# A hybrid encoder block: gate-up weight sums all formed at once, another order of its seven products, and an output projection in 512 columns

## The chip, the cores and the metric

The kernel runs on one core of a Trainium2 chip. The metric is the device time of one execution in microseconds (us), the median of the runs shown. The engines are named TensorE (PE), VectorE (DVE), ScalarE (ACT), GpSimd (POOL) and SyncE (SP, which here only issues DMAs).

## The reference

One layer of a trunk, on x of 2048 tokens by 1024 channels, everything in float32:

```python
h  = rms_norm(x, norm_mix)
u  = h @ w_in                                   # (2048, 2560): lru_x, lru_g, q, k, v of 512 each
y_lru = gelu(lru_g) * rg_lru(conv4(lru_x), ...) # a gated linear recurrence over time
y_att = stick_breaking_attention(q, k, v)       # 8 heads of 64, causal, no softmax
y  = concat([rms_norm(y_lru), rms_norm(y_att)])
x  = x + y @ w_out                              # output projection, 1024 x 1024
h2 = rms_norm(x, norm_ffn)
gu = h2 @ w_ffn_in                              # gate-up projection, 1024 x 5632
x  = x + (silu(gu[:, :2816]) * gu[:, 2816:]) @ w_ffn_out   # down projection
out = rms_norm(x, norm_final)
```

## The kernel before

**Precision.** Each operand of a large product is split into a high part (`hi`, a cast by ACT to the type fp32r) and a low part (`lo`, source minus `hi`, a subtraction by DVE or POOL). `mm3` (L149 to L151) then issues three multiplications for each block: hi by hi, hi by lo, lo by hi. A split therefore always means a cast on ACT and a subtraction on DVE or POOL (`split` with its flag `pool`).

**Stages.** The span runs through these stages. First, for each of four groups of 512 tokens, the input projection of the next group goes on beside the attention of the present one (`drive` hands steps of the one between steps of the other). In the last group, from 801 to 1208 us, the output projection of all groups takes the place of the input projection (`mix_out`, class `Mix`); its last part, the tail, runs after attention, to about 1242. In the tail the tokens for the gate-up projection are prepared too (`prep_tokens`, L801). Then the gate-up projection (44 quads, about 1250 to 2172), and then the down projection to the end.

**Output projection.** `Mix.run` (L657) takes, for each 512 columns of the output, two half blocks of weights from `next_half`. A half is 256 columns wide and holds all four channel blocks of a branch. For each of four token tiles it fills one bank of PSUM, left half and then right half, in 8 x 3 multiplications of 256 columns; it yields four times on the way, so that attention steps can come between.

**Gate-up by Strassen's scheme.** Weights and tokens are cut into 2 x 2 blocks (a11, a12, a21, a22 and b11, b12, b21, b22, where the first index of a and b runs over outputs and channels of the scheme), and seven products of sums replace eight. The weight sums are s1 to s4, the token sums t1 to t4; `ORDER` (L64) pairs them and sets the order of the products. Each product is 4 row blocks x 3 multiplications of 512 columns, in one of four banks a to d (each with two buffers). Of one `quad`: product 0 (a11, b11) goes to bank a and is copied out by ACT as p; a later product is added on top of it in bank a and copied out as u; DVE adds u to bank c as the second u ("u3" in the code); and bank c and then d are filled further after DVE has read them. `use` adds a bank and one of the copies into an activation tile c; for the even quads ACT applies silu to it, for the odd ones DVE multiplies it with the gate of the quad before, and POOL forms five sums of such tiles (e), which go to DRAM (act_d) as operands of the down projection.

**Weights of the next quad.** `prep_weights` (L893) is a generator. `done(i)`, called after product i of the present quad, lets it take one step for the next quad. Its six steps: the split of the first raw block (a11 and a12 together, 1024 wide, subtraction on POOL); the sums s3 and s1, and the split of s3 (POOL); the sum s2 and its split (DVE); the split of s1 (DVE); the split of a22 (POOL) and the sum s4, formed in place in s2; the split of s4 (POOL) and the issue of the loads of the quad after (`load_weights`, two raw blocks of 512 KB, L885). There is one pair of raw buffers, so the next load starts when their last reader is through. Split weights live in a ring of six buffers (`WSB`), a11 and a12 in two double-width ones.

**Tokens.** `EARLY` names the five token operands that are prepared in the tail; the other two follow in the gate-up stage, ahead of the first quad. `turns_late` prepares the second half of the tokens beside the first half's quads: transposes on PE, and sums t1 to t4 on POOL that go to DRAM. At the swap of halves `split_tokens` loads and splits 7 x 4 token tiles, each after the product that used the old one.

**Order of the work.** PE's instructions are issued in the order of the program (`manual_schedule`). The other engines, and SP, get an order from a planner, which takes the instruction that is ready first by its own estimate of times, and among ready ones the one that stands first in the program. On the chip every engine then works in that order, whatever really comes first: an instruction that waits holds all behind it.

## Time and profile before

| | |
|---|---|
| time, median of 3 runs | 2612.49 us (2610.23 to 2614.08) |
| profiled execution | 2616.12 us, of which the span of instructions is 2614.4 us |
| PE, matmul | 2417.2 us busy, 92% |
| PE, weight load | 2046.0 us busy, 78% |
| DVE | 1837.1 us busy, 70% |
| ACT | 1258.0 us busy, 48% |
| POOL | 1174.2 us busy, 45% |
| DMA | 468.57 MB, mean 179 GB/s |
| granted clock of TensorE, mean | 0.970 |

A clock of 1.00 is 2.4 GHz; the other level is 1.2 GHz, and a value between them is a mean over time at both. A busy share is an average over stages with different limits, so the rows below are taken by stretch of time (us from the start of the span). Multiplications are pipelined: one of 512 columns is recorded with 0.39 us, but the next one starts well before that has passed, so the step from start to start is what counts.

### The profile page before, as it was taken

The page shows a single profiled execution, that of the slowest core. Times are in us where ns is not written, and L with a number is a line of the kernel's source. Part 1 is how long each engine was busy: PE and PEld are TensorE (multiplying, and loading weights), DVE is VectorE, ACT ScalarE, POOL GpSimd, SP SyncE. Part 2 cuts the span into 40 slices and gives each one's busy share as a digit, 9 for nine tenths or more (in the row PEclk, how much of TensorE's full clock was granted, in tenths as well). Part 3 has the DMA queues.
Part 4 walks back from the last instruction along what each step waited for, and adds up shares of the span by engine and source line. Part 5 has one row for each costly group of instructions (what it writes and reads, how often), then busy time and mean ns, then how long its engine had stood idle before and what let it go on. Part 6 is the DMA issues. An engine that isn't in the chain of part 4 may idle for free.

```text
span 2614.4 us, 36856 instructions
## 1 busy us (share of the span) xinstructions
PE 2417.2 (92%) x12680; PEld 2046.0 (78%) x12680; DVE 1837.1 (70%) x2569; ACT 1258.0 (48%) x2277; POOL 1174.2 (45%) x1397
## 2 busy tenths in 40 slices
PE   7999999998888887998799979979999999999998
PEld 5888788787778787888577758868888887788886
DVE  4566888999999999898645546686566562544557
ACT  5656677676766665665433323343333332332334
POOL 5855433223244221112565565464555454644443
PEclk9999999999999999999899989989999999999999
DMA  7787887664556565654333453252332326755563
GB/s 254 254 289 254 268 264 228 197 210 164 163 182 204 176 200 174 218 177 138 128 133 129 150 196 110 90 199 89 109 113 93 102 92 263 272 174 173 195 200 145
DMA packets 221804, 468.57 MB, mean 179 GB/s; under 512 B 22704, under 2 KB 63664, under 8 KB 221616
## 3 DMA queue, kind: packets, MB, share of 16 engines
q1 hardware_dynamic: 221616, 466.21, 53.1%
q8 instruction: 100, 1.64, 0.3%
q14 instruction: 88, 0.72, 0.1%
HBM read 333.74 MB, written 132.38 MB: 178 GB/s over the span
## 4 chain that ended last, share of the span: by engine, by line
PE 43%; DVE 3%; DMA 2%; POOL 2%; issue 2%; ACT 1%; SPq 0%; POOLq 0%; DVEq 0%; ACTq 0%
PE pw L151 5%; PE pw L150 5%; PE pw L149 5%; PE psc L149 3%; PE psa L149 3%; PE psc L150 3%; PE psc L151 3%; PE psa L150 3%; PE psa L151 3%; PE psd L149 3%; PE psd L150 3%; PE psd L151 3%; PE psb L149 1%; PE psb L150 1%; PE psb L151 1%
## 5 line engine op out<-in xcount | busy, mean ns | idle before, releaser
L360 POOL MEMSET u<- 128x1 f32 x320 | 31.2, 99 | 558.0 <-DVE u L372 393.4
L372 DVE TENSOR_TENSOR_SCAN u<-u,u,zero 128x513 f32<-128x513 f32 x192 | 255.5, 1332 | 9.0 <-ACT u L362 8.5
L393 PE MATMUL t<-ident,be 128*128 128x128 f32 x1088 | 180.2, 282 | 55.2 <-DVE al L395 46.2
L378 DVE TENSOR_TENSOR be<-be,u 128x512 f32<-128x512 f32 (+2 forms) x320 | 215.2, 675 | 17.0 <-POOL be L366 1.4
L362 ACT ACTIVATE u<-z 128x512 f32<-128x512 f32 (+2 forms) x320 | 172.4, 539 | 96.8 <-PE z L358 61.2
L149 PE MATMUL pj<-ht_hi,w_hi 128*128 128x512 f32 x512 | 214.9, 420 | 2.3 <-DVE sl L291 1.5
L394 ACT CAST ah<-t 128x512 fp32r<-128x512 f32 (+2 forms) x320 | 168.7, 527 | 87.0 <-PE t L393 81.6
L393 PEld LDWEIGHTS t<-ident,be 128*128 128x128 f32 x1088 | 131.7, 144 | 94.1 <-DVE al L395 60.5
L151 PE MATMUL pj<-ht_hi,w_lo 128*128 128x512 f32 x512 | 202.3, 395 | 0.0
L150 PE MATMUL pj<-ht_lo,w_hi 128*128 128x512 f32 x512 | 202.0, 395 | 0.0
L358 PE MATMUL z<-ks,qd 128*128 128x512 f32 (+2 forms) x640 | 191.1, 380 | 6.8 <-ACT be L363 5.2
L395 DVE TENSOR_TENSOR al<-t,ah 128x512 fp32r<-128x512 f32 (+2 forms) x320 | 191.1, 598 | 7.1 <-ACT ah L394 6.7
L1089 POOL TENSOR_TENSOR e<-c,c 128x512 f32<-128x512 f32 x110 | 158.7, 1451 | 50.5 <-DVE c L1080 36.8
L363 ACT ACTIVATE be<-z 128x512 f32<-128x512 f32 (+2 forms) x320 | 172.6, 539 | 0.2
L408 PE MATMUL y<-ah,vs 128*128 128x256 f32 x576 | 149.6, 290 | 13.9 <-DVE yp L418 13.9
L149 PE MATMUL po<-wo_hi,yhi 128*128 128x256 f32 x512 | 156.3, 305 | 0.0
L372 DVE TENSOR_TENSOR_SCAN u<-u,zero 128x129 f32<-128x129 f32 (+3 forms) x128 | 112.1, 877 | 57.0 <-POOL u L366 55.4
L1142 DVE TENSOR_TENSOR blo<-dr,bhi 128x1024 fp32r<-128x1024 f32 (+1 forms) x41 | 83.1, 2029 | 94.5 <-ACT bhi L1141 94.5
L1142 POOL TENSOR_TENSOR a0lo<-act,a0hi 128x1024 fp32r<-128x1024 f32 (+1 forms) x41 | 99.4, 2424 | 110.6 <-ACT a0hi L1141 110.6
L408 PE MATMUL y<-al,vs 128*128 128x256 f32 x576 | 147.2, 286 | 0.0
L150 PE MATMUL po<-wo_lo,yhi 128*128 128x256 f32 x512 | 146.6, 286 | 0.0
L151 PE MATMUL po<-wo_hi,ylo 128*128 128x256 f32 x512 | 146.6, 286 | 0.0
(283 smaller groups left out, 7564.3 us busy)
## 6 DMA issues: line engine op xcount, KB each, us to landing
r<-in_w_gu SPq DMA_DIRECT2D x88, 512.0 KB, 4.1
act<-act_d SPq DMA_DIRECT2D x68, 512.0 KB, 4.1
dr<-in_w_dn SPq DMA_DIRECT2D x59, 512.0 KB, 4.5
act_d<-e SPq DMA_DIRECT2D x110, 256.0 KB, 2.0
w_hi<-w_d SPq DMA_DIRECT2D x50, 512.0 KB, 4.7
w_lo<-w_d SPq DMA_DIRECT2D x50, 512.0 KB, 5.6
vs<-vs_d SPq DMA_DIRECT2D x80, 256.0 KB, 3.6
ks<-ks_d SPq DMA_DIRECT2D x80, 256.0 KB, 3.6
```

Source lines behind the costliest of these rows:

```text
L149: nc.tensor.matmul(ps, lhsT=w_hi, rhs=m_hi, start=first, stop=False, skip_group_check=more)
L150: nc.tensor.matmul(ps, lhsT=w_hi, rhs=m_lo, start=False, stop=False, skip_group_check=more)
L151: nc.tensor.matmul(ps, lhsT=w_lo, rhs=m_hi, start=False, stop=last, skip_group_check=more)
L358: nc.tensor.matmul(z[:, :nz], lhsT=qd[:, i, qs], rhs=kss[p.c][:, :nz], start=i == 0, stop=i == 1)
L362: nc.scalar.activation(u[:, :n], z[:, :n], AF.Sigmoid, scale=-SCALE)
L363: nc.scalar.activation(be[:, :n], z[:, :n], AF.Sigmoid, scale=SCALE)
L372: nc.vector.tensor_tensor_scan(out=ur, data0=ur, data1=zero.broadcast_to([P, n + 1]), initial=1.0 if p.prev is None else p.prev.u[s][:, 0: ...
L378: nc.vector.tensor_tensor(out=p.be[s][:, :n], in0=p.be[s][:, :n], in1=p.u[s][:, 1:n + 1], op=ALU.mult)
L393: nc.tensor.transpose(tp[:, b, :], p.be[s][:, b * P:(b + 1) * P], ident)
L395: nc.vector.tensor_tensor(out=alo[:, :nb, s, :], in0=tp[:, :nb, :], in1=f32(ahi[:, :nb, s, :]), op=ALU.subtract)
L408: nc.tensor.matmul(y, lhsT=vs[:, b, :], rhs=t[:, b].rearrange("p s q -> p (s q)"), start=first and m == 0, stop=last and m == 1)
L1142: eng.tensor_tensor(out=lo, in0=src, in1=f32(hi), op=ALU.subtract)
```

## The change

The weight sums of a quad are formed in the first two steps of `prep_weights` instead of over five of them; a22 gets buffers of its own and is split in the second step, and the loads of the quad after are issued there too. The products come in another order: the one that takes a12 and b21 is now second, in bank b, and its `use` follows at once. b21 changes places with t4 in `EARLY`: t4 is formed in the tail, stored to DRAM, and loaded and split later. For the very first quad a11 and a12 are loaded and split at the end of the tail, in buffers of the pool of token tiles. Pools: split weights 6 to 5 buffers (and two new ones for a22), weight sums 3 to 4, copies p/u 3 to 2, activation tiles 8 to 6. In the output projection a half of the weights is 512 columns by two channel blocks instead of 256 by four, and a multiplication has 512 columns. The raw loads of w_in and w_out are written with flat patterns.

```diff
-WSB = 6
-CB = 8
+WSB = 5
+CB = 6
-ORDER = (("a11", "b11"), ("s3", "t3"), ("s2", "t2"), ("s1", "t1"), ("a22", "t4"), ("s4", "b22"), ("a12", "b21"))
-EARLY = ("b11", "t1", "t2", "t3", "t4")
+ORDER = (("a11", "b11"), ("a12", "b21"), ("s3", "t3"), ("s2", "t2"), ("s1", "t1"), ("a22", "t4"), ("s4", "b22"))
+EARLY = ("b11", "b21", "t3", "t2", "t1")
...
     def run(self, x2, following=None, ready=NCT):
             for n in range(D // GT):
-                halves = [next_half(), next_half()]
+                halves = [[w.rearrange("p (a k) c -> p a (k c)", a=2) for w in next_half()] for _ in range(2)]
...
-                    for i, (hi, lo) in enumerate(halves):
-                        for c in range(NCT):
-                            yh, yl = self.split[c]
-                            mm3(po[:, i * WC:(i + 1) * WC], yh[:, ts], yl[:, ts], hi[:, c], lo[:, c],
-                                c == 0, c == NCT - 1)
-                            if c == 1 or (c == NCT - 1 and i == 0):
-                                yield
+                    for c in range(NCT):
+                        yh, yl = self.split[c]
+                        hi, lo = halves[c // 2]
+                        mm3(po, yh[:, ts], yl[:, ts], hi[:, c % 2], lo[:, c % 2], c == 0, c == NCT - 1)
+                        if c < NCT - 1:
+                            yield
...
@@ prep_tokens
-                    b11, b12, b22 = load(0, 0), load(0, 1), load(1, 1)
+                    b11, b12, b22, b21 = load(0, 0), load(0, 1), load(1, 1), load(1, 0)
                     split("b11", kk, b11, True)
+                    split("b21", kk, b21, True)
...
-                    b21 = load(1, 0)
                     nc.vector.tensor_tensor(out=b21, in0=b21, in1=b22, op=ALU.subtract)
-                    split("t4", kk, b21, False)
+                    nc.sync.dma_start(out=t4_d[kk], in_=b21)
                 else:
+                    t4 = prp.tile([P, GT], F32, tag="r", name=f"t4_{half}_{kk}")
+                    nc.sync.dma_start(out=t4, in_=t4_d[kk])
+                    split("t4", kk, t4, False)
                     split("b22", kk, load(1, 1), True)
-                    split("b21", kk, load(1, 0), False)
...
+        w0 = {}
+        for j, q in enumerate(("a11", "a12")):
+            raw, hi, lo = (prp.tile([P, KD // 2, P], d, tag="r", name=f"{q}{x}_first")
+                           for x, d in (("r", F32), ("h", F32R), ("l", F32R)))
+            nc.sync.dma_start(out=raw, in_=w_gu[0, 0][:, j * KD // 2:(j + 1) * KD // 2])
+            nc.scalar.copy(hi, raw)
+            nc.vector.tensor_tensor(out=lo, in0=raw, in1=f32(hi), op=ALU.subtract)
+            w0[q] = hi, lo
...
@@ prep_weights
-            hi = wsp.tile([P, KD, P], F32R, tag="hi2", name=f"a1h{n}", bufs=2)
...
-            yield
+            if n:
+                hi = wsp.tile([P, KD, P], F32R, tag="hi2", name=f"a1h{n}", bufs=2)
...
             s3 = new("s3", a11, a21, ALU.subtract)
             s1 = new("s1", a21, a22, ALU.add)
+            yield
+            hi = wsp.tile([P, K2, P], F32R, tag="hi3", name=f"a22h{n}", bufs=2)
+            lo = wsp.tile([P, K2, P], F32R, tag="lo3", name=f"a22l{n}", bufs=2)
+            nc.scalar.copy(hi, a22)
+            nc.gpsimd.tensor_tensor(out=lo, in0=a22, in1=f32(hi), op=ALU.subtract)
+            w["a22"] = hi, lo
+            s2 = new("s2", s1, a11, ALU.subtract)
+            s4 = new("s4", a12, s2, ALU.subtract)
+            load_weights(n + 1)
+            yield
             split("s3", s3, True)
             yield
-            s2 = new("s2", s1, a11, ALU.subtract)
             split("s2", s2, False)
             yield
             split("s1", s1, False)
             yield
-            split("a22", a22, True)
-            nc.vector.tensor_tensor(out=s2, in0=a12, in1=s2, op=ALU.subtract)
-            yield
-            split("s4", s2, True)
-            load_weights(n + 1)
+            split("s4", s4, True)
             yield
...
@@ quad
             product("a", 0)
             p1 = keep("a", "p1")
             done(0)
-            product("c", 1)
+            product("b", 1)
+            use(0, 0, ps["b"], p1)
             done(1)
-            product("a", 2, True)
+            product("c", 2)
+            done(2)
+            product("a", 3, True)
             u2 = keep("a", "u2")
...
             nc.vector.tensor_tensor(out=u3, in0=ps["c"], in1=u2, op=ALU.add)
-            done(2)
-            product("d", 3)
+            done(3)
+            product("d", 4)
             use(1, 1, ps["d"], u3)
-            product("c", 4, True)
+            product("c", 5, True)
             use(1, 0, ps["c"], u2)
-            product("d", 5, True)
+            product("d", 6, True)
             use(0, 1, ps["d"], u2)
-            product("b", 6)
-            use(0, 0, ps["b"], p1)
```

## Rows read from the trace of the kernel before

**Rows 1.** Busy time by stretch: stretch, its length, each engine, PE clock, DMA

```profile
801.00:1208.00 407.00, 357.83 (x2643) 333.47 (x2643) 381.47 (x612) 251.81 (x513) 91.86 (x251) 0.95 0.55 184
1208.00:1242.00 34.00, 27.14 (x204) 26.73 (x202) 27.33 (x49) 17.14 (x36) 12.32 (x9) 0.85 0.56 174
1250.00:1284.00 34.00, 25.72 (x83) 19.30 (x84) 21.93 (x20) 15.50 (x26) 27.38 (x16) 0.78 0.32 108
1284.00:1700.00 416.00, 390.60 (x1687) 317.95 (x1687) 231.26 (x253) 132.87 (x209) 236.66 (x153) 0.96 0.39 132
1700.00:1800.00 100.00, 86.56 (x366) 69.58 (x365) 76.01 (x78) 43.18 (x73) 59.79 (x38) 0.93 0.46 156
1800.00:2150.00 350.00, 349.50 (x1532) 286.49 (x1531) 213.79 (x235) 117.12 (x183) 183.87 (x119) 1.00 0.31 103
2150.00:2215.00 65.00, 58.94 (x251) 47.93 (x250) 17.71 (x18) 18.46 (x22) 29.00 (x16) 0.95 0.59 220
```

**Rows 2.** PE's waits, 1242 to 1284: total us, times, longest

```profile
PE psd L149 <- ACT s3h L898: 5.7, 1, 5.7
```

**Rows 3.** PE's waits, 1284 to 1700

```profile
PE psa L149 <- ACT p L943: 20.0, 4, 10.5
PE psc L149 <- DVE u L955: 5.3, 4, 3.0
```

**Rows 4.** PE's waits, 1700 to 1800

```profile
PE psc L149 <- DVE u L955: 12.7, 2, 11.9
```

**Rows 5.** PE's waits, 2150 to 2215

```profile
PE pw L149 <- issue: 4.8, 1, 4.8
```

**Rows 6.** Timeline of PE: start, duration, engine, line, operation, wait before it

```profile
1222.01 0.28 PE L149 MATMUL po<-wo_hi,yhi 128*128 128x256 f32 x1
...
1241.33 0.28 PE L151 MATMUL po<-wo_hi,ylo 128*128 128x256 f32 x1
1250.12 0.79 PE L149 MATMUL psa<-b,a1h 128*128 128x512 f32 x1 [8.51 <-ACT a1h L909]
...
1264.55 0.39 PE L149 MATMUL psd<-t,s1h 128*128 128x512 f32 x1
...
1267.27 0.39 PE L149 MATMUL psc<-t,a22h 128*128 128x512 f32 x1
...
1284.27 0.39 PE L149 MATMUL psa<-b,a1h 128*128 128x512 f32 x1
```

**Rows 7.** DVE by line, 1250 to 2172: busy, mean ns, idle before

```profile
L904 DVE TENSOR_TENSOR s3s<-r,r 128x512 f32<-128x512 f32 x44 | 42.5, 965 | 109.9 <-DMA r<-in_w_gu 108.9 <-POOL s4l L899 0.9
```

**Rows 8.** Timelines of SP, DVE, ACT and PE around one long wait

```profile
1554.96 0.38 SPq L885 DMA_DIRECT2D r<-in_w_gu  x1
...
1558.81 0.69 DVE L904 TENSOR_TENSOR s3s<-r,r 128x512 f32<-128x512 f32 x1 [14.00 <-DMA r<-in_w_gu]
...
1562.07 0.57 ACT L943 COPY p<-psa 128x512 f32<-128x512 f32 x1
...
1562.69 0.80 PE L149 MATMUL psa<-t,s2h 128*128 128x512 f32 x1 [10.45 <-ACT p L943]
```

**Rows 9.** Timeline around u in a quad without waits

```profile
1379.32 0.69 DVE L955 TENSOR_TENSOR u<-psc,u 128x512 f32<-128x512 f32 x1
...
1380.80 0.39 PE L149 MATMUL psc<-t,a22h 128*128 128x512 f32 x1
```

**Rows 10.** DVE by line in the tail, 1208 to 1242

```profile
L813 DVE TENSOR_TENSOR t<-b,t 128x512 fp32r<-128x512 f32 x12 | 9.5, 793 | 1.3 <-ACT t L812 1.3
...
L829 DVE TENSOR_TENSOR b<-b,b 128x512 f32<-128x512 f32 x3 | 4.1, 1369 | 0.0
```

**Rows 11.** Timeline at the end of the gate-up stage

```profile
2177.36 1.29 POOL L1089 TENSOR_TENSOR e<-c,c 128x512 f32<-128x512 f32 x1 [0.90 <-DMA act_d<-e]
2180.82 0.38 SPq L1127 DMA_DIRECT2D dr<-in_w_dn  x1
```

**Rows 12.** Timeline at the start of the gate-up stage

```profile
1249.02 1.04 ACT L909 CAST a1h<-r 128x1024 fp32r<-128x1024 f32 x1 [5.73 <-issue]
```

More of the change, by code (lines that the diff above doesn't have):

```diff
@@ L113, in tile_block @@
                dram.tile([P, GT], F32, name=f"{q}_d{k}") for k in range(KD // 2)] for _, q in ORDER}
+    t4_d = [dram.tile([P, GT], F32, name=f"t4_0_d{k}") for k in range(KD // 2)]
     NPAIR = NF // 2
@@ L224, in load_half @@
         raw = wp.tile([P, KD // 2, WC], F32, tag="w_raw", name=f"{name}_raw", bufs=2)
-        nc.sync.dma_start(out=raw, in_=src)
+        nc.sync.dma_start(out=raw.rearrange("p k c -> p (k c)"), in_=src.rearrange("p k c -> p (k c)"))
         nc.scalar.copy(hi, raw)
@@ L252, in tile_block @@
         for br in range(2):
-            for n in range(D // WC):
-                queue.append((w_out[n][:, br * KD // 2:(br + 1) * KD // 2], f"wo{g}_{br}_{n}", ("out", br, n), g < NG - 1))
+            for n in range(D // GT):
+                for i in range(2):
+                    k0 = br * KD // 2 + i * KD // 4
+                    queue.append((w_out[n][:, k0:k0 + KD // 4], f"wo{g}_{br}_{n}_{i}", ("out", br, n, i), g < NG - 1))
     loaded, taken = [], []
@@ L874, in tile_block @@
         wsp = uctx.enter_context(tc.tile_pool(name="wsp", bufs=WSB, side="left"))
-        tmp = uctx.enter_context(tc.tile_pool(name="tmp", bufs=3, side="left"))
+        tmp = uctx.enter_context(tc.tile_pool(name="tmp", bufs=2, side="left"))
         K2 = KD // 2
@@ L902, in new @@
             def new(q, x, y, op):
-                t = wrp.tile([P, K2, P], F32, tag="s", name=f"{q}s{n}", bufs=3)
+                t = wrp.tile([P, K2, P], F32, tag="s", name=f"{q}s{n}", bufs=4)
                 nc.vector.tensor_tensor(out=t, in0=x, in1=y, op=op)
                 return t
-            hi = wsp.tile([P, KD, P], F32R, tag="hi2", name=f"a1h{n}", bufs=2)
-            lo = wsp.tile([P, KD, P], F32R, tag="lo2", name=f"a1l{n}", bufs=2)
-            nc.scalar.copy(hi, r[0])
-            nc.gpsimd.tensor_tensor(out=lo, in0=r[0], in1=f32(hi), op=ALU.subtract)
-            w["a11"], w["a12"] = (hi[:, :K2], lo[:, :K2]), (hi[:, K2:], lo[:, K2:])
-            yield
+            if n:
+                hi = wsp.tile([P, KD, P], F32R, tag="hi2", name=f"a1h{n}", bufs=2)
+                lo = wsp.tile([P, KD, P], F32R, tag="lo2", name=f"a1l{n}", bufs=2)
+                nc.scalar.copy(hi, r[0])
+                nc.gpsimd.tensor_tensor(out=lo, in0=r[0], in1=f32(hi), op=ALU.subtract)
+                w["a11"], w["a12"] = (hi[:, :K2], lo[:, :K2]), (hi[:, K2:], lo[:, K2:])
             s3 = new("s3", a11, a21, ALU.subtract)
             s1 = new("s1", a21, a22, ALU.add)
+            yield
[8 more added lines that the diff above has]
+            yield
             split("s3", s3, True)
             yield
-            s2 = new("s2", s1, a11, ALU.subtract)
             split("s2", s2, False)
@@ L955, in quad @@
             nc.vector.tensor_tensor(out=u3, in0=ps["c"], in1=u2, op=ALU.add)
-            done(2)
-            product("d", 3)
+            done(3)
+            product("d", 4)
             use(1, 1, ps["d"], u3)
-            done(3)
-            product("c", 4, True)
+            done(4)
+            product("c", 5, True)
             use(1, 0, ps["c"], u2)
-            done(4)
-            product("d", 5, True)
+            done(5)
+            product("d", 6, True)
             use(0, 1, ps["d"], u2)
-            done(5)
-            product("b", 6)
-            use(0, 0, ps["b"], p1)
             done(6)
@@ L1041, in first_step @@
                 if i >= CH:
-                    n = "" if i == CH else ""
-                    dst.append([wsp.tile([P, GT], F32R, tag=f"{x}{n}", name=f"a{x}_first{i}") for x in ("hi", "lo")])
+                    n = "3" if i == CH else ""
+                    dst.append([wsp.tile([P, GT], F32R, tag=f"{x}{n}", name=f"a{x}_first{i}",
+                                         bufs=2 if n else WSB) for x in ("hi", "lo")])
                 hi, lo = dst[i]
@@ L1054, in tile_block @@
         load_weights(0)
-        ahead = {}
+        ahead = dict(w0)
         for _ in prep_weights(0, ahead):
@@ L1244, in _lay_out @@
         "w_in": cols(w_in[0], WC),
-        "w_out": cols(w_out[0], WC),
+        "w_out": cols(w_out[0], GT),
         "w_gu": w_gu,
```

## The prediction

> **What bounds the kernel now.** I read the busy times by stretch first, then what TensorE (PE) waited for in each stretch, then the order of time around each wait. A multiplication of 512 columns follows the one before it after 2.72 us / 12 = 0.227 us (the first of a product at 1264.55, of the next at 1267.27), one of 256 columns after 0.120 us (161 steps from 1222.01 to 1241.33) [rows 6]. From that: a product of the gate-up stage (4 row blocks, 3 multiplications each) costs 2.72 us, a quad (7 products) 19.0, all 44 quads 838 us. The stage begins at 1250.1, and PE stood for 8.51 us before it [rows 6].
>
> The reader is to see that the loss isn't spread evenly. From 1800 to 2150 PE is busy for 349.50 of 350 us at clock 1.00: there is nothing to win. The loss is in four places, by the waits of each stretch and its clock [rows 1 to 6]:
> - Start: 8.5 us of waiting for the first weights, and a first quad of 34.15 us (1250.12 to 1284.27) where 19.0 would do, so 15.1 more. Together 23.6, of which 5.7 is one wait before the s4 product; the clock of the stretch is 0.78, so a good part ran at 1.2 GHz instead of 2.4.
> - 1284 to 1700: 20.0 us of waits for p (the copy of the first product out of its bank) and 5.3 for u (the sum that frees bank c), and clock 0.96: 0.04 x 416 = 16.6 us. Together 41.9.
> - 1700 to 1800, where the tokens of the second half are split: 12.7 us of waits for u and 0.07 x 100 = 7 by the clock. Together 19.7.
> - End: 4.8 us until the down projection's second step has its data, and 0.05 x 65 = 3.3 by the clock. Together 8.
>
> Behind the waits from 1284 to 1800 stands one cause. VectorE (DVE) idled 108.9 us in front of the sum s3 until the raw weights landed, and what queues behind s3 on DVE, or behind its cast on ScalarE (ACT), is p and u. The worst case: the second raw load is issued at 1554.96, s3 starts at 1558.81 after 14.00 us of idle DVE, p runs at 1562.07, and PE resumes at 1562.69 after 10.45 [rows 7, 8]. The load is late because the raw buffers are given back late: their last readers (the split of a22 on GpSimd (POOL), the sum s4 on DVE) come after the fourth product, and SP issues loads in order behind stores that wait for POOL.
>
> **The change part by part.** All against the profiled execution (2616.1 us, span 2614.4), which is 3.6 above the median of the three runs, 2612.5.
>
> *Output projection in 512 columns.* 1536 multiplications of 256 columns become 768 of 512: 1536 x 0.120 - 768 x 0.227 = 10 us of PE. One eighth lies in the tail after attention, where PE is the last to finish: 192 x 0.120 - 96 x 0.227 = 1.3 us, taken in full. The other 9 us lie in 801 to 1208, where DVE is busy 381.47 of 407 us [rows 1]; its work doesn't change, and the number of steps handed to attention doesn't either. I take 2 (0 to 9). By the Trainium skill (TensorE: Matmul & The Clock Gate, Back-to-back issue gap) only some 2.5 ns per removed multiplication would go, an estimate of 0.2 us in the tail; the rows show 13 ns per pair, and the rows decide. The loads of w_out and the flattened transfer move the same bytes, two halves ahead: 0.
>
> *Start.* The halves a11 and a12 of the first block are now loaded and split during the tail, in buffers of the token pool, so the first two products need neither the new pools nor the 8.5 us. I let them start at 1242.0 and end at 1247.4. What is next late is s3: its raw blocks still wait for the tail's buffers and land at 1249.0 (the cast of the first block, which waits for them, starts at 1249.02 [rows 12]). Then come the sum (0.7), its cast (0.6, as p) and a POOL split (1.3) that may stand behind that of a22, about 3 us in all, so the third product runs fully from 1252.2. The rest of it and four products are 13.1 us, 2.5 more at the lower clock: the quad ends at 1267.8 instead of 1284.27, -16.5. The wait of 5.7 goes because the next raw load no longer stands behind late POOL work: both sums and the a22 split come first, so the buffers are free some 10 us earlier. Bounds: -23 if nothing waits, -6 if the late tokens t4 and b22, which now wait for the six buffers that the first weights hold until the second product, cost again what s4 cost. In the tail itself the split of t4 leaves DVE (4 x 0.7), the splits of a11 and a12 come (2 x 0.7), and four splits of b21 come to POOL. POOL beside DVE is not free: in the tail POOL has nine operations [rows 1], and two groups of DVE there mean 793 and 1369 ns [rows 10] where one undisturbed took 690 [rows 9]: 12 x 0.10 + 3 x 0.68 = 3.2 us for nine, so four more cost 1.4; this is within the 16.5. The Trainium skill (GPSIMD Engine Reference, Specifications) says that the two engines share their SBUF interfaces and collide when DVE reads two SBUF inputs, as all these do; if each new POOL split held DVE for its full length, that would be an estimate of 5 us and a total nearer 2554.
>
> *1284 to 1700.* Two things act. First, the product order: p has two products until bank a is needed again (5.4 us instead of 2.7). If data came as late as now, 2.7 off each of the four p waits (the longest 10.5) would leave at best 20.0 - 4 x 2.7 = 9.2. Second, the weights: the load after next is issued at the second step of a quad instead of the sixth, four products or 10.9 us earlier, against a longest wait of 14.0. And a12, now second instead of last, gives its buffer back five products earlier. With both I leave 4 us of waits and 5 by the clock of the 41.9: -33 (bounds -8 and -42). The order between u and bank c is as before, one product: u ends at about 1380.0 and bank c is taken at 1380.80 [rows 9], 0.8 us of spare.
>
> *Swap of halves.* DVE is busy 76 of 100 us there [rows 1], and the 21 token splits that it does of the 28 stay. Only the raw load and p improve: -7 of 19.7 (bounds -18, and +10 if b21, now due at the second product, comes late).
>
> *1800 to 2150.* No gain is left. The smaller pools (six activation tiles, two of p/u, five split buffers) could cost: the copy p now takes the buffer of the old u, which DVE frees with one sum (0.7 us) after the last product, and p comes 2.7 us after it. 0; the price if it fails is a rival below.
>
> *End.* The last block of a quad now feeds two sums instead of three; the last sum started at 2177.36 and the load behind it at 2180.82 [rows 11]. Two such sums fewer at 1.3 us each on POOL, and PE's wait shrinks from 4.8 to about 2.3, with a little clock: -3 (-1 to -6).
>
> Sum: -1.3 - 2 - 16.5 - 33 - 7 + 0 - 3 = -62.8; 2616.1 - 62.8 = 2553.3, less 3.6: 2550.
>
> **The rivals.**
> - *The loads stay late.* PE alone has a fixed order; the other engines are ordered by readiness in a plan, so asking for a load earlier need not issue it earlier, and SP still has POOL's stores in front. For it: POOL's sums for the second half from 1500 to 1560 remain. Then p's added room alone acts (at most 10.8 of waits, 3 of clock: -14), the start gives -12, the end -2, the swap 0: with the 3.3 of the output projection -31, so 2581.
> - *All waits go.* -3.3 - 21.5 - 42 - 18 - 5 = -90: 2523. Against it: DVE's 21 splits at the swap.
> - *Slower: u falls behind a raw wait.* Place: DVE's queue between the fourth product and u. The sums now run nearly a quad ahead, so the s3 of a later block can stand in front of u. Price: the wait in front of s3 is 109.9 / 44 = 2.5 us on the mean [rows 7], 0.8 of it has cover [rows 9], so 1.7 x 44 = 75 us. Against only start, end and output projection (-22.8) it decides from 0.52 us per quad on; in full it gives 2612.5 - 22.8 + 75 = 2665. For it: from 1284 to 1700 u was late four times. Against it: the load would now land around a quad's first product, 8 us ahead of u.
>
> **How the numbers follow.** Forecast 0.58, late loads 0.20, all waits gone 0.15, slower 0.05, nothing left over 0.02. The range reaches from just above the "all gone" case to beyond the late loads: 2526 to 2588; below and above lie about one in ten each. Differences under 0.2% (5 us) can't be told from none here. Faster 0.93, same 0.02, slower 0.05.
>
> **What would show it.** Right: the first product within a few us of the tail's last multiplication; no wait for a first-block cast; the s4 product of the first quad without a wait of 5 us; p nearly gone from PE's waits from 1284 on; clock 0.98 or more there; the end's wait near 2 us. Wrong: DVE's idle time in front of s3 followed by u as PE's releaser in many quads, a first quad still over 28 us, or waits at the swap that grow.

## The result and the profile after

The changed kernel takes 2584.22 us (median of 4 runs, 2582.70 to 2586.40), the kernel before took 2612.06 beside it: ratio 0.9892 [0.9876, 0.9908], 28 us gained where 62 were forecast. The profiled execution (2582.70, span 2581.0) lost 33.4 us of span against the profiled one of before; some 5 of these are the spread of executions, since the profiled one of before (2616.12) was 4 above its median and this one 1.5 below. Cut at the first multiplication of each quad (the first `psa` row after the last `psd` or `psb` row of the timeline), by the prediction's steps:

| step | before, us | after, us | change | forecast |
|---|---|---|---|---|
| to the tail's last multiplication | 1241.6 | 1233.9 | -7.7 | -3.3 |
| from there to quad 1 (start) | 42.7 | 41.2 | -1.5 | -16.5 |
| quads 1 to 19 (1284 to 1694 before) | 410.2 | 391.1 | -19.1 | -33 |
| quads 20 to 23 (swap) | 93.4 | 92.4 | -1.0 | -7 |
| quads 24 to 43 | 384.5 | 382.7 | -1.8 | 0 |
| after the last quad | 442.1 | 439.7 | -2.4 | -3 |

The windows of the gate-up stage of the kernel after, columns as in [rows 1], cut to its own stages:

```profile
1242.00:1276.00 34.00, 23.50 (x77) 17.80 (x76) 28.21 (x29) 17.42 (x28) 28.68 (x16) 0.80 0.52 181
1276.00:1700.00 424.00, 407.68 (x1801) 333.86 (x1799) 234.73 (x274) 146.67 (x231) 256.47 (x165) 0.98 0.41 140
1700.00:1800.00 100.00, 90.31 (x375) 73.74 (x375) 70.86 (x79) 38.43 (x64) 58.84 (x36) 0.93 0.44 150
1800.00:2130.00 330.00, 329.71 (x1450) 271.40 (x1449) 181.87 (x219) 112.34 (x174) 173.70 (x111) 1.00 0.28 98
```

PE's waits of the same kernel (total us, times, longest), from 1238 to 1276, 1276 to 1700, 1700 to 1800 and 2130 to 2200:

```profile
PE psc L150 <- DVE u L976: 5.8, 1, 5.8
PE psc L150 <- ACT s3h L911: 4.1, 1, 4.1
PE psa L150 <- ACT sqf L697: 3.7, 1, 3.7
...
PE psc L150 <- DVE u L976: 12.3, 6, 9.1
PE h2t L1003 <- POOL hn L995: 4.0, 3, 1.4
...
PE psc L150 <- DVE u L976: 9.7, 2, 5.6
...
PE pw L150 <- issue: 2.5, 1, 2.5
PE pw L152 <- POOL a0lo L1161: 1.7, 1, 1.7
```

Against [rows 2 to 5]: the s4 wait at the start (5.7), all p waits (20.0) and half of the end's wait are gone. But u's waits grew from 5.3 to 12.3 between the start and 1700, waits for hn (POOL's scaling of tokens ahead of their transposes) are new there with 4.0, u now has one in the first quad, and at the swap 9.7 of 12.7 remain.

The start, on PE's timeline of the kernel after (last multiplication of the tail, first of gate-up, of s3, of a22, of quad 1):

```profile
1233.52 0.39 PE L152 MATMUL po<-wo_hi,ylo 128*128 128x512 f32 x1
...
1237.61 0.47 PE L150 MATMUL psa<-b,a11h_first 128*128 128x512 f32 x1 [3.70 <-ACT sqf L697]
...
1249.04 0.79 PE L150 MATMUL psc<-t,s3h 128*128 128x512 f32 x1 [4.08 <-ACT s3h L911]
...
1266.85 0.80 PE L150 MATMUL psc<-t,a22h 128*128 128x512 f32 x1 [5.81 <-DVE u L976]
...
1275.12 0.39 PE L150 MATMUL psa<-b,a1h 128*128 128x512 f32 x1
```

DVE's queue in front of that u, whose input (the ACT copy) was there from about 1260.4 on:

```profile
1252.98 3.46 DVE L815 TENSOR_TENSOR t<-t,t 128x512 fp32r<-128x512 f32 x2
1256.37 2.88 DVE L917 TENSOR_TENSOR s3s<-r,r 128x512 f32<-128x512 f32 x1
1259.18 1.78 DVE L815 TENSOR_TENSOR t<-t,t 128x512 fp32r<-128x512 f32 x1
1260.88 1.75 DVE L917 TENSOR_TENSOR s1s<-r 128x512 f32<-128x512 f32 x1
1262.66 1.06 DVE L917 TENSOR_TENSOR s2s<-s1s,r 128x512 f32<-128x512 f32 x1
1263.82 0.69 DVE L917 TENSOR_TENSOR s4s<-r,s2s 128x512 f32<-128x512 f32 x1
1264.43 1.76 DVE L815 TENSOR_TENSOR t<-t,t 128x512 fp32r<-128x512 f32 x1
1266.12 0.68 DVE L976 TENSOR_TENSOR u<-psc,u 128x512 f32<-128x512 f32 x1
```

The four sums of the next block (6.4 us together) and the four late splits of t4 stand ahead of u, and none has a gap.

DVE by line over the quads (busy, mean ns, idle before and its releasers), answering [rows 7]:

```profile
L917 DVE TENSOR_TENSOR s3s<-r,r 128x512 f32<-128x512 f32 x44 | 42.6, 968 | 138.9 <-DMA r<-in_w_gu 136.5 <-POOL s3l L912 2.4
L917 DVE TENSOR_TENSOR s4s<-r,s2s 128x512 f32<-128x512 f32 x44 | 35.0, 796 | 31.1 <-POOL s4l L912 30.8
```

DVE's idle time in front of the first sum didn't shrink, it grew from 108.9 to 136.5 us. That isn't a later load. On the mean of quads 1 to 19 the second raw load of a quad is now issued 38.8 us ahead of the quad's first multiplication and lands 34.1 ahead; before, it was issued 25.7 and landed 21.4 ahead. So the data come 13 us earlier, but s3s moved up by as much (33.7 us ahead of its quad, 21.2 before), and DVE stands in front of it as it did. Quad 12 as an example: its two loads on SP, s3s on DVE and its first multiplication, in the kernel before and then in the kernel after:

```profile
1489.39 2.24 SPq L885 DMA_DIRECT2D r<-in_w_gu  x2
...
1496.39 0.69 DVE L904 TENSOR_TENSOR s3s<-r,r 128x512 f32<-128x512 f32 x1 [2.96 <-DMA r<-in_w_gu]
...
1517.83 0.39 PE L149 MATMUL psa<-b,a1h 128*128 128x512 f32 x1
```

```profile
1460.12 1.62 SPq L898 DMA_DIRECT2D r<-in_w_gu  x2
...
1466.46 0.69 DVE L917 TENSOR_TENSOR s3s<-r,r 128x512 f32<-128x512 f32 x1 [3.28 <-DMA r<-in_w_gu]
...
1501.05 0.39 PE L150 MATMUL psa<-b,a1h 128*128 128x512 f32 x1
```

And s4, formed "at once" in the program, waits 30.8 us for POOL to give back the buffer of an earlier sum. The longest wait of the kernel after, the counterpart of [rows 8], shows both on the timelines of POOL, DVE, SP, ACT and PE:

```profile
1502.82 1.29 POOL L912 TENSOR_TENSOR s4l<-s4s,s4h 128x512 fp32r<-128x512 f32 x1
...
1504.14 1.76 DVE L917 TENSOR_TENSOR s4s<-r,s2s 128x512 f32<-128x512 f32 x1 [6.79 <-POOL s4l L912]
...
1505.32 1.74 POOL L932 TENSOR_TENSOR a22l<-r,a22h 128x512 fp32r<-128x512 f32 x1
...
1509.00 2.02 SPq L1110 DMA_DIRECT2D act_d<-e  x2
...
1511.12 0.38 SPq L898 DMA_DIRECT2D r<-in_w_gu  x1
...
1514.77 2.67 DVE L917 TENSOR_TENSOR s3s<-r,r 128x512 f32<-128x512 f32 x1 [5.24 <-DMA r<-in_w_gu]
...
1518.07 0.63 ACT L1096 ACTIVATE c<-c 128x512 f32<-128x512 f32 x1 [7.13 <-DVE c L1094]
...
1523.20 0.68 DVE L976 TENSOR_TENSOR u<-psc,u 128x512 f32<-128x512 f32 x1
1523.93 0.79 PE L150 MATMUL psc<-t,a22h 128*128 128x512 f32 x1 [9.12 <-DVE u L976]
```

POOL's s4l is late behind three token sums for the second half. So s4s is late, and so is the split of a22 behind s4l on POOL, the last reader of the second raw block. That block's buffer is given back late, its next load is issued late (behind two stores on SP), and s3s waits for it. Behind s3s, in order, stand the sum c, on ACT the activation that waits for that c (7.13 us) with the casts and the copy for u after it, and then u. The load isn't late for its own quad, which is quad 14 and begins at 1551.47: what is late is the u of quad 12, behind work for quad 14.

### The profile page after: what moved, and what is told of

It is laid out like the page before. It is cut to its first block, busy times and chain, and to the rows that moved or that the text cites. A ratio compares the mean times of both kernels' runs of the same rounds, so it can differ in the third digit from the quotient of the medians.

```text
span 2581.0 us, 35351 instructions
## 1 busy us (share of the span) xinstructions
PE 2402.4 (93%) x11912; PEld 1995.3 (77%) x11912; DVE 1802.7 (70%) x2567; ACT 1259.2 (49%) x2278; POOL 1186.1 (46%) x1400
## 5 line engine op out<-in xcount | busy, mean ns | idle before, releaser
L363 POOL MEMSET u<- 128x1 f32 x320 | 30.8, 98 | 545.5 <-DVE u L375 378.8
L411 PE MATMUL y<-ah,vs 128*128 128x256 f32 x576 | 148.5, 289 | 12.7 <-DVE yp L421 12.6
L924 POOL TENSOR_TENSOR a1l<-r,a1h 128x1024 fp32r<-128x1024 f32 x43 | 115.1, 2678 | 82.6 <-ACT a1h L923 78.8
L361 PEld LDWEIGHTS z<-ks,qd 128*128 128x128 f32 x640 | 117.5, 193 | 29.1 <-ACT be L366 6.4
L917 DVE TENSOR_TENSOR s3s<-r,r 128x512 f32<-128x512 f32 x44 | 42.6, 968 | 138.9 <-DMA r<-in_w_gu 136.5
```

The costliest lines, as they stand in the source:

```text
L361: nc.tensor.matmul(z[:, :nz], lhsT=qd[:, i, qs], rhs=kss[p.c][:, :nz], start=i == 0, stop=i == 1)
L411: nc.tensor.matmul(y, lhsT=vs[:, b, :], rhs=t[:, b].rearrange("p s q -> p (s q)"), start=first and m == 0, stop=last and m == 1)
```

## The experiments

Each kernel was compared with the kernel before on the same chip: median, and ratio with its 95% interval. Stretches are those of the table above; "start" runs from the tail's last multiplication to quad 1.

### The parts alone

**e1_out512**: the kernel before with the output projection of the kernel after.

```diff
-            for n in range(D // WC):
+            for n in range(D // GT):
+                for i in range(2):
...
-        "w_out": cols(w_out[0], WC),
+        "w_out": cols(w_out[0], GT),
```

> The kernel before with the output projection's part of the change alone (512 columns, the layout of w_out, the flat transfer). The prediction gave it -3.3 us (attention -2, tail -1.3). The two traces show the tail's last multiplication 7.7 us earlier in the kernel after. If that is the output projection's own, this kernel gains 6 to 9 us (2603 to 2606); if the 7.7 us come from the token work of the tail, it gains 3 or less.

2608.15, 0.9990 [0.9981, 0.9999]: 2.3 us (0.3 to 5.0 by the interval), the small value. In its profile the tail ended 6.6 earlier; 1.3 of that went into the first wait (9.8 instead of 8.5) and 3.0 into the stretch after the last quad.

**e2_gateup**: the kernel after with the reverse of that edit.

> The kernel after with the output projection of the kernel before, so the gate-up part of the change alone. Theory (gains add): 2584.2 plus what the other run takes off, so 2591 if the output projection is worth 7, 2587 if it is worth 3. Rival (the two hide each other: a tail that ends earlier only waits longer for weights and tokens at the start of gate-up): within 2 us of the kernel after, 2584 to 2586.

2599.16, 0.9953 [0.9941, 0.9966]. Neither: the part alone gains 11, not 21 to 25. So 2 + 11 make 28 together.

**e3_order**: e2 with the preparation of before and without the early first weights.

```diff
-        w0 = {}
-        for j, q in enumerate(("a11", "a12")):
...
+            yield
+            s2 = new("s2", s1, a11, ALU.subtract)
+            split("s2", s2, False)
...
+            split("s4", s2, True)
+            load_weights(n + 1)
```

> The kernel before with only the product order, the early tokens and the buffer counts that go with them (5 split buffers, six activation tiles, two of p and u); the sums are formed one by one as before, the load is asked for at the sixth step as before, the first weights come by the common way, the output projection is that of before. Theory (the sums formed at once bring no earlier load, p's added room is what acted): the waits for p are gone all the same, and the quads from the second on take within 5 us of what they take in the kernel after; with the first weights' 8 us wait still there, the time is 2592 to 2602. Rival (forming the sums at once is what brought the gain): 2605 or more, with PE waits of 10 us and more left between 1284 and 1700.

2594.22, 0.9935 [0.9922, 0.9947]: the theory's range, and the quads from 1 on take 867.1 us, the kernel after 866.2. The product order with its tokens and buffer counts (no run parts these) brings some 16 us, more than half of everything, and is 5 faster than e2, which has the sums at once and the early weights besides. The waits for p, expected to go, are more than halved (9.5 us, [rows 3] has 20.0), although the second raw load lands only 15.0 us ahead of its quad here, later than before (21.4).

**h2_w0_order** (e3 with the early weights) and **h3_out_order** (e3 with 512 columns) complete the table.

> The kernel before with the new product order, tokens and the early first weights, but the sums one by one and the output projection of before. With 512 columns the same kernel took 2586.3. Theory (the output projection is worth what it is alone, 2 to 6 us): 2588 to 2592. Rival (it is worth 15 us with any new gate-up, as between the gate-up part alone and the kernel after): 2600 to 2602.

> The kernel with the order alone (2594.2) and the output projection in 512 columns: no early first weights, sums one by one. Theory (2 to 6 us for the output projection): 2588 to 2592. Rival (15 us): 2578 to 2581, which would be faster than the kernel after.

2593.38, 0.9929 [0.9916, 0.9941], and 2586.85, 0.9905 [0.9891, 0.9919]. Medians of all with the new order, in us:

| | 256 columns | 512 columns |
|---|---|---|
| sums one by one, no early weights | 2594.2 (e3) | 2586.9 (h3) |
| sums one by one, early weights | 2593.4 (h2) | 2586.3 (f1) |
| sums at once, no early weights | not run | 2587.4 (g4) |
| sums at once, early weights | 2599.2 (e2) | 2584.2 (after) |

With the sums one by one the output projection is worth 7 us (h2 and h3 each missed their theory's range by 1), the early weights about 1, which the intervals don't tell from none. The sums at once are worth 2 with 512 columns and the early weights and nothing without these, again within the intervals, and cost 6 with 256. Why just there isn't settled: in e2's profile quad 1 has a u wait of 4.0 us that the kernel after doesn't have, with DVE's operations in the same order in both from that quad on.

### Sums at once, early weights

**f1_oldprep**: the kernel after with the preparation of before (the added lines of e3).

> The kernel after with the weight preparation of the kernel before: the sums formed one by one, the split of a22 at the fifth step, the load asked for at the last; product order, first weights, tokens and output projection stay those of the kernel after. The kernel with the order alone was 5 us faster than the gate-up part as a whole, so theory: forming the sums at once gains nothing and costs some 5 us, and this kernel takes 2576 to 2581. Rival (that 5 us came from the first weights, which hold the token buffers): this kernel is within 2 us of the kernel after or slower, 2583 to 2588.

2586.27, 0.9901 [0.9887, 0.9914]: the rival, 2 us slower, which the intervals don't tell from none. By stretches two things cancel: start 35.4 (41.2 after: -5.8), quads 1 to 19 402.5 (391.1: +11.4), swap 89.3 (92.4: -3.1), quads 24 to 43 381.0 (382.7: -1.7). So the sums at once, with the loads that they let start earlier (the second one lands 14.2 us ahead of its quad here, 34.1 in the kernel after), do gain 11.4 where the forecast said, and lose 10.6 at three places.

**g4_now0**: the kernel after without the early first weights.

```diff
-        w0 = {}
...
-        ahead = dict(w0)
+        ahead = {}
```

> The kernel after without the early first weights: the first block comes by the common way, with the split of its first half on POOL, as in the kernel before. Theory (the early weights are worth the wait for the first cast, which was 8.5 us before and 3.7 after, and a part of the first quad): the first wait is 9 to 12 us again and the time 2588 to 2592. Rival (the six token buffers that the first weights hold delay t4 and b22, and DVE loses two splits, which costs as much as is won): 2582 to 2586.

2587.36, 0.9908 [0.9895, 0.9922], between the two. The first wait is 10.5 us again (3.7 after), but the first quad takes 30.9 instead of 37.5: the start is 41.4 against 41.2. The 6.8 us won at the first wait were lost again within the quad.

**g1_hybrid**: sums at once for blocks 2 to 19 only.

```diff
+            if n not in ONCE:
...
+                return
```

> The kernel after with the sums formed at once only for blocks 2 to 19 (prepared in quads 1 to 18); the first two blocks and those from the 20th on are prepared one sum at a time, as in the kernel before. By the stretches of the kernel with the old preparation throughout: it won 5.8 us in the first quad, 3.1 at the swap and 1.7 behind it, and lost 11.4 in the quads 1 to 19. Theory (forming the sums at once gains where loads are late and costs where DVE is full, and the two places are independent): -9 to -11 against the kernel after, 2573 to 2576. Rival (the gains of the early quads come with the later form's other buffers and order, so a mixture gets neither): within 3 of the kernel after, 2581 to 2587.

2585.55, 0.9905 [0.9890, 0.9920]: the rival. The start is 35.3, the swap 89.1, as hoped; but the u wait moved into quad 1, which takes 28.9 us instead of 19.5. PE's wait in this kernel, 1240 to 1300:

```profile
PE psc L152 <- DVE u L996: 6.7, 1, 6.7
```

**g3_right**: gate-up's PSUM banks from the other end.

```diff
-name="ps_u", bufs=2, space=PSUM, side="left"
+name="ps_u", bufs=2, space=PSUM, side="right"
```

> The kernel after with gate-up's PSUM banks allotted from the other end, so that the first banks are not those from which the tail is still being read. The first multiplication now waits 3.70 us behind the tail's last. Theory (that wait is for the tail's last sum to leave the bank): the wait falls under 1 us and the first quad starts 3 us earlier; how much of it stays depends on what is next late, s3, which now waits 4.1 us: if that wait grows by the same 3 us, the time stays 2583 to 2585; if not, 2580 to 2582. Rival (the wait is for the data of the first weights): the wait stays.

2588.23, 0.9910 [0.9896, 0.9923]; the wait stayed, as the rival has it:

```profile
1241.64 0.76 PE L150 MATMUL psa<-b,a11h_first 128*128 128x512 f32 x1 [3.74 <-DVE xo L673]
```

It ends when the tail's last two sums on DVE end (1240.10 plus 1.40), behind two splits; the data of the first weights had been there since about 1240.2, so the rival's reason is wrong too. What ties the first product to those sums isn't settled, nor whether the edit moved it off their bank: gate-up's four banks have two buffers each, and no run shows which of them the tail used last.

### Loads, POOL's queue, DVE's queue

**e5_noload**: no loads after the first quad's.

```diff
-            if n < len(jobs):
+            if 0 < n < len(jobs):
+                raws[n] = raws[0]
+            elif n < len(jobs):
```

> The kernel after, with the raw weights of the first quad serving all 44: the loads of the other 43 are left out, every other instruction stays (so what is computed is not the reference's). No sum can then wait for a load. Theory (late loads hold the sums up, and u, bank c's release, stands behind the sums on DVE): the PE waits for u between 1400 and 1700 (11 to 12 us) go and 4 us of the clock with them; the time falls to 2566 to 2572. Rival (u is late because DVE has too much to do there, or because of POOL's sums for the second half): the waits for u stay within 4 us of what they are, and the time stays above 2578.

2578.78, 0.9875 [0.9862, 0.9889]: 5 us, the rival, by a hair (2578 was its bound). Quads 1 to 10 take 198.7 (205.7 after), so loads do cost there; but the long u wait is still there. Timelines of DVE and PE:

```profile
1508.11 1.73 DVE L919 TENSOR_TENSOR s3s<-r,r 128x512 f32<-128x512 f32 x1 [12.07 <-POOL s3l L914]
...
1515.81 0.79 PE L150 MATMUL psc<-t,a22h 128*128 128x512 f32 x1 [10.26 <-DVE u L978]
```

With its raw data in place, the sum s3 waits 12.07 us for POOL, which does token sums and activation sums before the split that frees the buffer.

**f2_sumsdve**: those 16 token sums on DVE.

```diff
-                    nc.gpsimd.tensor_tensor(out=t, in0=x, in1=y, op=ALU.subtract)
+                    nc.vector.tensor_tensor(out=t, in0=x, in1=y, op=ALU.subtract)
```

> The kernel after with the second half's token sums (16 subtractions) on DVE instead of POOL. With no loads at all a u came 10.3 us late at 1516 us, and DVE's s3s had waited 12.1 us there for POOL's s3l, behind these sums. Theory (POOL's queue is behind the wait: a sum waits for a buffer that a late POOL split still reads, and u waits behind the sum on DVE): the wait of 9.1 us near 1524 goes, with the clock that falls after it 10 to 12 us; 2572 to 2576. Rival (loads or DVE's own load are behind it): the wait stays or grows, 2583 or more.

2583.77, 0.9889 [0.9874, 0.9904]: by the time the rival, no gain; by the wait the theory. The 9.1 us wait is gone (1.1 there) and quads 11 to 19 take 180.4 instead of 185.4, but DVE now makes u 4.1 late one quad earlier, and in the profiled execution the attention ended 4.8 us later, with the same order of its work.

**h1_noload_dve**: both edits.

> The kernel after with both the second half's token sums on DVE and the raw weights of the first quad serving all 44 (the loads of the other 43 are left out, so what is computed is not the reference's). Quads 1 to 19 took 391.1 us in the kernel after, 385.8 with the sums on DVE, 382.7 without loads. Theory (late loads and POOL's queue are two causes that add): 377 to 379 us for these 19 quads and no wait for u in them over 1 us; total 2568 to 2576. Rival (one cause behind both, a full DVE queue): a wait for u of 4 us or more is left there, and the 19 quads take 382 or more.

2577.68, 0.9868 [0.9852, 0.9884], a little outside either text: quads 1 to 19 take 379.5, where 391.1 is the kernel after; the two causes nearly add there (8.4 and 5.3 alone, 11.6 together). A u wait of 5.3 us is left all the same, and at the swap 96.8 us (92.4) are spent; that the sums, no longer held back by loads, stand there in front of u is likely, but no run parts it.

**g5_s4dve**: the split of s4 on DVE.

```diff
-            split("s4", s4, True)
+            split("s4", s4, False)
```

> The kernel after with the split of s4 on DVE instead of POOL. This split, the last reader of a sum's buffer, stands behind POOL's token sums and activation sums; DVE waited 6.8 us for it at 1504 us. Theory (POOL's queue holds the sum buffers and with them DVE): the wait of 9.1 us near 1524 shrinks to under 4, and with the clock 5 to 8 us go: 2576 to 2579; the quads from 1800 on don't change (DVE is busy 55 per cent of the time there). Rival (another split on DVE stands in front of u as well): the waits for u at the start and at the swap grow by 2 us or more each, and the time is 2584 or more.

2593.47, 0.9930 [0.9917, 0.9944]: the rival by the time, 9 slower, but not at its places: u's wait at the start fell from 5.8 to 4.1, those at the swap rose only from 9.7 to 10.7. The wait of 9.1 became 6.1 and 4.6 in two quads, and from 1800 to 2130, where the kernel after has 0.3 us of waits:

```profile
PE psc L150 <- DVE u L976: 5.2, 8, 1.3
```

**f3_dveorder** and **h5_behind_u**: DVE in program order, the sums ahead of u and, in h5, behind it (its four sums and the load are moved from the first two steps to the fourth).

```diff
-    with tc.manual_schedule(engines={mybir.EngineType.PE}), up_r,
+    with tc.manual_schedule(engines={mybir.EngineType.PE, mybir.EngineType.DVE}), up_r,
```

> The kernel after with DVE of the gate-up stage in the order of the program instead of the planner's: the four sums of the next block ahead of u, the splits of s2 and s1 behind it. Theory (u is late by what stands in front of it on DVE, the next block's sums, which wait for POOL's splits and for loads): all four sums stand in front of each u now, so waits for u appear in many quads and the time grows to 2600 to 2680. Rival (the splits s2l and s1l in front of u are what delays it): the waits shrink and the time falls under 2580.

> The kernel after with DVE of gate-up in the order of the program and the four sums, formed at once, placed directly behind u instead of ahead of it (the load after next is asked for behind them, at the fourth step). The mirror of the kernel with DVE in program order and the sums ahead of u (2593.5). Theory (u is late by what stands in front of it on DVE): between 1300 and 1680 no wait for u over 1 us, the quads 1 to 19 take 377 to 382 us instead of 391.1, and the first quad loses its 5.8 us wait; 2568 to 2576. Rival (the program's order on DVE costs by itself, since stores, activations and token splits then wait for loads): waits of other kinds take their place, 2585 or more.

f3: 2593.51, 0.9926 [0.9914, 0.9939], under the theory's range; from 1300 to 1680 u is late in seven quads (19.3 us; five and 11.5 in the kernel after), not in many. h5: 2593.09, 0.9932 [0.9918, 0.9945], by the time the rival. Its u is never late from 1300 to 1680, as its theory says, but the time goes to others. PE's waits in that stretch, then from 1800 to 2130:

```profile
PE psd L150 <- DVE c L1095: 5.2, 9, 2.3
PE psc L152 <- POOL s3l L912: 3.6, 1, 3.6
...
PE psd L150 <- DVE c L1095: 5.3, 17, 0.7
```

The sums now stand in front of c, which frees bank d one product later. Quads 24 to 43 take 392.7 instead of 382.7.

**f4_swap2**: token splits at the swap 14 and 14.

```diff
-                (nc.gpsimd if kk == 1 else nc.vector)
+                (nc.gpsimd if kk % 2 else nc.vector)
```

> The kernel after with the token splits at the swap of the halves shared evenly, 14 on DVE and 14 on POOL instead of 21 and 7. Theory (at the swap u is late because DVE is full): the two waits for u of 4.1 and 5.6 us near 1704 and 1732 fall to 3 together, the stretch's clock rises, -6 to -9: 2575 to 2578. Rival (POOL, 58 of 100 us busy there and in order, then holds up the splits of s3 and s4 and through their buffers DVE): the waits stay or grow, 2582 to 2590.

2589.84, 0.9914 [0.9901, 0.9928]: the rival by time, 6 slower, the two waits 14.7 instead of 9.7. But not by POOL's queue alone. In front of the first late u DVE did the same five operations as in the kernel after, now beside a busy POOL, in 8.4 us (1699.66 to 1708.04) instead of 4.1 (1699.43 to 1703.51). One of them and u, in f4 and then in the kernel after:

```profile
1703.03 1.75 DVE L917 TENSOR_TENSOR s1s<-r 128x512 f32<-128x512 f32 x1
...
1708.04 0.68 DVE L976 TENSOR_TENSOR u<-psc,u 128x512 f32<-128x512 f32 x1
```

```profile
1701.71 0.68 DVE L917 TENSOR_TENSOR s1s<-r 128x512 f32<-128x512 f32 x1
...
1703.51 0.68 DVE L976 TENSOR_TENSOR u<-psc,u 128x512 f32<-128x512 f32 x1
```

And this although DVE was busy for less in all: 58.4 us from 1700 to 1790, 62.9 in the kernel after.

### A version from the stretches

**i1_mixed**: g1 with `ONCE = range(20)`, and f2's edit. **i2_mixed_hn**: i1 with the 16 hn on ACT.

```diff
-                    nc.gpsimd.tensor_scalar(out=ht, in0=ht, scalar1=rsf[...], scalar2=None, op0=ALU.mult)
+                    nc.scalar.activation(ht, ht, AF.Copy, scale=rsf[...])
```

> A version put together from the stretches: the kernel after, with the sums at once for blocks 0 to 19 only (old preparation from the 20th on, which won 3.1 us at the swap and 1.7 behind it) and the second half's token sums on DVE (which won 5.0 in quads 11 to 19). If the stretches add: -9 to -10 against the kernel after, 2574 to 2576. Rival (a wait that is taken away at one place returns at another, as in the mixture before): within 3 of it, 2581 to 2587.

> The same with the 16 scalings hn (1.64 us each on POOL, 26 us in all) on ACT, which is busy about a third of the time there. Theory (POOL's queue is what holds the transposes, 4.0 us of waits near 1390, and part of the clock): another -4 to -6, 2569 to 2572. Rival (on ACT they stand in front of p, u and the casts, and wait there for their loads): the wait goes to p or u, no gain, 2574 to 2580 or more.

2577.11, 0.9863 [0.9846, 0.9879], and 2577.40, 0.9862 [0.9848, 0.9877]. Both beat both kernels; i1 is 7 us under the kernel after (2575.7 to 2579.6 against 2582.7 to 2586.4), near its theory. Its profile, of the slowest of its runs, shows 3 of these: the swap (-2.5) and the quads behind it (-1.7), with a tail that ended 1.5 later. Quads 1 to 19 are nearly as in the kernel after (390.4): of f2's 5.0 us in quads 11 to 19 only 2.1 are there, and quads 1 to 10 take 1.4 more. i2 is the rival: the hn waits (4.0 us) are gone, and u's from 1280 to 1800 grew from 18.7 to

```profile
PE psc L152 <- DVE u L996: 23.7, 7, 6.1
```

## Why the prediction came out wrong

Direction right, size wrong: 28 us for 62. The terms, in the prediction's order:

- *Output projection, -3.3.* The term was too small: 7 us by two pairs of kernels with the new order (2.3 in the kernel before, 15 with everything). The profiles place it ahead of gate-up: the tail's last multiplication comes at 1232.5 to 1238.7 us in every kernel with 512 columns, at 1241.6 to 1248.0 with 256.
- *Start, -16.5.* **This is the step that failed**: "The rest of it and four products are 13.1 us", so "the quad ends at 1267.8". It ended at 1275.12, although the tail before it ended 7.7 us earlier; the start gained 1.5, so 15.0 were missed. The s3 product ran fully from 1250.87, near the 1252.2 of the forecast, but that is luck: behind the tail's end it came 17.0 us and not 10.6, and the raw blocks it was reckoned from landed by 1246.0 and not at 1249.0. So 6.4 us were missed ahead of it and 8.6 behind it. There the working counted products with no wait, and u came 5.81 us late: the next block's four sums and the late t4 splits, made ready early by the change itself, stood ahead of it on DVE. Taking the early sums away (f1) gives 5.8 us of the start back; taking the early weights away (g4) changes the start by 0.2. Three smaller misses: the first product came 3.7 us behind the tail's end and not 0.4; s3's cast was held on ACT; and PE's clock fell to about 0.5 (1.2 GHz) three times, from 1238.5 to 1242 (0.52), from 1249 to 1255 and from 1267 to 1272 (0.50 each), each time behind one of the three long waits (3.7, 4.1 and 5.8 us). (ACT at s3, in the kernel after: the first activation, which the new order makes due after the second product, and the table load for it stand ahead of the cast.)

```profile
1246.55 1.28 ACT L1096 ACT_TABLE_LOAD   x1
1247.85 0.63 ACT L1096 ACTIVATE c<-c 128x512 f32<-128x512 f32 x1
1248.38 0.60 ACT L911 CAST s3h<-s3s 128x512 fp32r<-128x512 f32 x1
```

- *1284 to 1700, -33.* Half wrong: -19.1. The product order did what was said of it and more: p's waits 20.0 to 0. The earlier load came too, 13 us where 10.9 were forecast. What failed is "With both I leave 4 us of waits and 5 by the clock": 16.3 us of waits (u 12.3, hn 4.0) and about 8.5 by the clock (0.02 x 424) were left. The sums moved up with the loads, so DVE's idle time in front of them stayed, now ahead of the u of an older quad; and s4 waits besides for one of four sum buffers that POOL's splits hold. The rival "the loads stay late" was given 0.20, and its 2581 is 3 from the result; but that is luck, since its loads are not what came, and it had -12 for the start and -14 here. Nor are the loads the whole of it: without any load, 8.4 of the stretch goes, and the 10.3 us wait is left (e5).
- *Swap, -7.* -1.0. The forecast put the waits there down to the raw weights too. But before the longest of them (11.94 us, ended at 1758.07 in the kernel before) s3s ran at 1744.40 without idle time, and DVE was busy from there up to u: it was full, and stayed so. The early sums cost 3.1 there on top (f1), and a swap without any load is worse still (96.5 in e5).
- *1800 to 2150, 0, and end, -3.* -1.8 and -2.4, close to the forecast; no wait for the u/p buffers shows. The end's wait fell from 4.8 to 2.5, and a POOL split follows with 1.7 (1.2 before).
- *The slower rival* named the right mechanism, u behind a sum that waits on DVE, and its price held (s3s waits 138.9 / 44 = 3.2 us per quad, 2.5 was assumed). But u pays for it in few quads: 22.3 us of waits from 1276 to 2130 (18.4 from 1284 to 2150 before), not 75. From 1800 to 2130 s3s waited 48.2 us for its data and PE 0.3: nothing behind it was due.
- In the sum of "All waits go", start and end stand with 21.5 and 5, where their own bounds are 23 and 6; by these it would be 2520. Nothing hangs on it.

Of what was to show the forecast right, five signs came (the first product near the tail, no wait before s4, no wait for p, clock 0.98, the end's wait near 2), and of those against it the first quad over 28 us, with 37.5.

What the runs show as a whole: from the start to the swap PE waits for one pair of in-order queues, DVE and POOL, tied by the sum buffers and by ACT's copies between them. The tie is read from the traces; no run gave the sums a fifth buffer, or moved the loads up and left the sums where they were. The forecast credited each wait separately as if its removal left the rest in place. Taken away at one point, the wait came back at another: from quad 0 to quad 1 (g1), from u to c (h5), from 1524 to 1503 (f2), from hn to u (i2).

## What to carry to other kernels

When a change makes work ready earlier, list what it will now stand in front of on each in-order engine, above all the small operation that frees an accumulator bank, and price the first round apart from the steady one: here the same edit gained 11.4 us in nineteen quads and lost 5.8 in the first. A load that comes earlier leaves the wait for it in place where the operation that waits moves up by as much in an in-order queue: look at what is due behind that operation now. And of several waits behind the same two queues only a part can be summed.

## What the runs showed of the hardware

DVE's 128x512 sums and splits with two operands from SBUF take 0.68 to 0.69 us while POOL is idle, and up to about 1.75 us, some more, beside a POOL operation; those that read a bank of PSUM take 0.68 to 0.69 us either way. Over the quads of the kernel after, 87 products of two activation tiles (c with c, both in SBUF) took 1.11 us on the mean, 87 sums of bank d and u 0.69. So work moved from DVE to POOL can slow what DVE keeps (f4). The Trainium skill (GPSIMD Engine Reference, Specifications) states that the two share their SBUF interfaces, with contention for DVE instructions with two SBUF inputs; the traces agree, and give the size, a factor of up to about 2.5. (The prediction took its undisturbed 690 ns from u, which reads a bank; s3s in [rows 8], with two operands from SBUF, gives the same.)

The same instruction order doesn't fix the time of the attention stage: with equal orders its last multiplication ended at 1233.9 us (the kernel after) and at 1238.7 (f2), so a stretch of one profile ahead of the gate-up stage can't be read to better than some 5 us.
